# A decoder block on one core: at most six gathers in flight in the routed stage, no dots in its first groups, two activation tables asked for elsewhere, and small moves between engines

## The chip, the cores and the metric

The kernel runs on one core of a Trainium2 chip. The metric is the device time of one execution in microseconds (us). A core has five engines with a queue of instructions each: PE (TensorE, matrix products), DVE (VectorE), ACT (ScalarE), POOL (GpSimd) and SP, which here only issues transfers. Each engine runs its own row of instructions in order and waits on semaphores for the others. Sixteen DMA engines move data between HBM and the core's memory; transfers whose rows are picked by an index list (gathers) are issued by POOL.

## The reference, cut to what matters

One block on x of 256 tokens with 2048 columns: a projection, sparse attention beside a convolution, an output projection, a layer norm that gives y, and a channel mixer that picks 16 experts for each of 8 heads (128 choices per token) out of 128 x 128, and a second layer norm. The change touches the mixer and the two norms:

```python
def peer_ffn(y, wq, sub_keys, u_tab, v_tab):
...
        q = (yb @ wq).reshape(bsz, PEER_BLOCK, PEER_HEADS, 2, PK_HALF)
        s1 = jnp.einsum('bthd,hkd->bthk', q[..., 0, :], sub_keys[:, 0])
        s2 = jnp.einsum('bthd,hkd->bthk', q[..., 1, :], sub_keys[:, 1])
        v1, i1 = lax.top_k(s1, PK_TOPK)
        v2, i2 = lax.top_k(s2, PK_TOPK)
...
        top, pos = lax.top_k(cand, PK_TOPK)
        eidx = jnp.take_along_axis(cidx, pos, axis=-1)
        g = jax.nn.softmax(top.astype(jnp.float32), axis=-1)
        u = u_tab[eidx]
        v = v_tab[eidx]
        h = jax.nn.gelu(jnp.einsum('btd,bthkd->bthk', yb, u))
        return jnp.einsum('bthk,bthkd->btd', g * h, v).astype(y.dtype)
...
        ffn = peer_ffn(x, peer_wq[l], peer_keys[l], peer_u[l], peer_v[l])
        x = layer_norm(DN_ALPHA * x + ffn, ln2_g[l], ln2_b[l])
```

## The kernel before, in words

The work runs in stages, each with its own loop; times are those of the profiled execution.

1. *Front*, to 365 us: projection, attention, convolution. The change leaves it alone.
2. *y stage*, 365 to 390: the first layer norm by blocks of columns (the helpers called from L1320 to L1385), its transposes `yh` and `yl` for PE, made on ACT and DVE from PE's bank `yt`, the transposed keys `keyT`, and the first matmuls with wq (bank `pwq`). `prime` is a tile of one element per partition, written by small activations only.
3. *wq stage*, 390 to 480 (loop over h from L1395): queries and scores per head, the short lists, and from head 3 on the first gathers, as many as there are free buffers (L1431).
4. *Dense u stage*, 480 to 900 (loop over j = 0 to 127, L1567): `u_mult(j)` makes with 27 matmuls (L1473, L1474, L1477) the product of a dense part of all rows u (1152 columns) with y for one key; `u_keep` (L1480) copies it from PE's bank to W on ACT. The other 896 columns are gathered: `gather(i)` (L1125, POOL) fetches for each of 128 tokens the row of its i-th choice (i = 0 to 255: 128 choices by two token blocks), and `dot(i)` (L1135, DVE) multiplies it with y and sums it into one column of `hv`. `dots_until` (L1168) sets both into the rows of POOL and DVE. When the first 128 are done, `swap` (L1453) copies the y row of the second token block to `yp`. The softmax of the gates (`gate_softmax`, L1087) is a generator, of which the loop takes a step per j; behind it two transposes (L1518) turn the gates into columns.
5. *Routed stage*, 900 to 1081. What belongs to a token's choices is picked out of W and put back by products with hot matrices. A group q (0 to 63) is four tokens: `ext_hot` (L1621, PE) and `ext_relu` (L1626, ACT) make the hot matrix in a `slot`, `ext_mask` (L1630, PE) and `ext` (L1635, PE) fill a `bank`, `ext_max` (L1639, DVE) reduces it to `top`. The groups run in pairs to QP = 36, then singly and together with the second half of the work (`sc_hot` L1665, `sc_relu` L1671, `sc_val` L1677, `sc` L1683, `sc_keep` L1689 and L1691), which runs 37 groups behind. The last 56 gathers and 59 dots lie beside this. `x_dots(q, n)` (L1816) is called once per group: it places dots until `done` reaches n, with every third as a multiplication on POOL (L1805) and, four groups on, a sum on ACT (L1815), and then issues gathers into all free buffers (L1829). The buffers are the remaining `gu`, and `moreh`, `morel`, `gx` and `spare`. `due(q)` (L1841) is n: it spreads the dots that are left over the groups, with twice the pace behind group 37. All this is written out in program order (a manual schedule): the order of the Python code is the order on each engine.
6. *Dense v stage*, 1081 to 1553 (loop over j, L1995): `vr`, the dense rows of v, are split on ACT, DVE and POOL into `vh` and `vl` (L1748, L1753) for PE (L329 to L331); the other 768 columns are gathered (`gv`, L1708) and summed into `pg` on DVE (L1713). `pg` begins as a copy of `gacc` (L2002).
7. *Tail*, 1553 to 1578 (L2036 to L2110): the second layer norm for two token blocks tt, each of four column blocks: three from PE's banks, and `nb`, of 768 columns, from `pg`. `center` and `shift` do one on DVE, `aside` one on ACT and POOL (L2066 to L2068), `stats` and `moments` the mean and variance, `send` the output (L2084, SP's queue).

## Time and profile before

| | us |
|---|---|
| median of 3 runs | 1575.16 (1574.26 to 1581.13) |
| profiled execution | 1579.51 |
| its span in the trace | 1577.7 |
| PE busy | 1518.9 (96%) |
| DVE busy | 1350.9 (86%) |
| POOL busy | 1058.8 (67%) |
| ACT busy | 888.4 (56%) |

A row of the timeline has the start in us from the span's start, the duration, the engine, the line, the operation, what it writes and reads, how many instructions were merged, and in brackets the idle time of the engine ahead of it with what ended that. PEld is PE's weight load, beside PE. "issue" means that the profile shows nothing that was waited for. The granted clock is the share of full speed that PE was allowed.

### The profile page before, as it was taken

What the parts mean: (1) busy time and instruction counts of PE and PEld (TensorE: products, weight loads), DVE (VectorE), ACT (ScalarE), POOL (GpSimd) and SP (SyncE); (2) the same over time, 40 slices, a digit from 0 to 9 for tenths busy, and PEclk for the clock granted to TensorE, in tenths of its full rate; (3) what the DMA queues carried; (4) which work ended last, traced back from release to release, by engine and by line L of the source; (5) the groups of instructions that cost most, each with busy time, mean ns of one, the idle gap of its engine ahead of it and who ended that gap; (6) DMA issues with size and microseconds to landing.
All of it is one profiled execution on the core that took longest, in us unless ns stands there. A gap on an engine that the chain in (4) does not pass through costs nothing. (4 is left out here: it accounts for less than half of the span.)

```text
span 1577.7 us, 29654 instructions
## 1 busy us (share of the span) xinstructions
PE 1518.9 (96%) x10932; PEld 1387.6 (88%) x10932; DVE 1350.9 (86%) x2438; ACT 888.4 (56%) x1270; POOL 1058.8 (67%) x908
## 2 busy tenths in 40 slices
PE   9999999999999999999999979999999999999996
PEld 9998999988999999999999967777888888788885
DVE  5999687756778999999997778878989899999997
ACT  5445766545336777777777636776344443434443
POOL 1886000064887777777776678747888888888884
PEclk9999999999999999999999989999999999999998
DMA  9663535364758999999999987647999999999996
GB/s 346 226 247 134 179 111 189 106 233 158 282 172 306 393 386 387 384 392 381 397 383 375 321 269 233 208 159 220 389 382 386 386 391 382 376 380 386 393 389 246
DMA packets 101349, 475.78 MB, mean 302 GB/s; under 512 B 17712, under 2 KB 20372, under 8 KB 92628
## 3 DMA queue, kind: packets, MB, share of 16 engines
q1 hardware_dynamic: 59444, 253.21, 43.7%
q0 software_dynamic: 41040, 218.60, 37.1%
q8 instruction: 85, 1.39, 0.4%
q10 hardware_dynamic: 720, 2.10, 0.3%
q14 instruction: 60, 0.49, 0.1%
HBM read 468.99 MB, written 4.85 MB: 300 GB/s over the span
## 5 line engine op out<-in xcount | busy, mean ns | idle before, releaser
L1708 POOL DMA_INDIRECT gv<-in_v_rows_dram,e x256 | 298.7, 1167 | 66.5 <-issue 41.1
L1748 ACT ACTIVATE vh<-vr 128x1280 fp32r<-128x1280 f32 (+1 forms) x129 | 162.1, 1258 | 275.0 <-DMA vr<-in_v_dense_dram 199.7
L290 POOL TENSOR_TENSOR lo<-raw,hi 128x1024 fp32r<-128x1024 f32 (+1 forms) x84 | 189.1, 2271 | 158.4 <-ACT hi L272 157.8
L1473 PE MATMUL hp<-yh,uh 128*128 128x256 f32 x1152 | 282.5, 283 | 2.8 <-ACT W L1480 2.5
L1474 PE MATMUL hp<-yl,uh 128*128 128x256 f32 x1152 | 281.9, 283 | 0.0
L1125 POOL DMA_INDIRECT gu<-in_u_rows_dram,e x200 | 193.9, 970 | 115.9 <-DVE gu L1135 73.0
L1713 DVE SCALAR_TENSOR_TENSOR pg<-gv,hv,pg 128x768 f32<-128x768 f32 x247 | 251.8, 1019 | 4.3
L1473 PEld LDWEIGHTS hp<-yh,uh 128*128 128x128 f32 x1152 | 221.1, 192 | 3.5 <-ACT W L1480 2.9
L1135 DVE SCALAR_TENSOR_TENSOR gu<-gu,yp 128x896 f32<-128x896 f32 x200 | 211.2, 1079 | 14.1 <-DMA gu<-in_u_rows_dram,e 14.0
L330 PE MATMUL f<-vl,wh 128*128 128x512 f32 x512 | 209.2, 409 | 13.1 <-DVE vl L1753 9.3
L1474 PEld LDWEIGHTS hp<-yl,uh 128*128 128x128 f32 x1152 | 221.1, 192 | 0.0
L272 ACT ACTIVATE hi<-raw 128x1024 fp32r<-128x1024 f32 (+1 forms) x134 | 138.2, 1036 | 136.8 <-issue 25.4
L1190 ACT ACTIVATE uh<-ur 128x1152 fp32r<-128x1152 f32 x128 | 149.5, 1168 | 103.2 <-issue 61.1
L329 PE MATMUL f<-vh,wh 128*128 128x512 f32 x512 | 203.9, 398 | 2.0 <-ACT vh L1748 1.8
L331 PE MATMUL f<-vh,wl 128*128 128x512 f32 x512 | 202.4, 395 | 0.0
L1753 DVE TENSOR_TENSOR vl<-vr,vh 128x1024 fp32r<-128x1024 f32 (+1 forms) x129 | 159.5, 1237 | 35.3 <-ACT vh L1748 25.6
L1477 PE MATMUL hp<-yh,ul 128*128 128x256 f32 x1152 | 159.2, 283 | 0.0
L1477 PEld LDWEIGHTS hp<-yh,ul 128*128 128x128 f32 x1152 | 147.5, 192 | 0.1
L1195 DVE TENSOR_TENSOR ul<-ut,uh 128x768 fp32r<-128x768 f32 x126 | 119.9, 952 | 23.9 <-issue 10.4
L330 PEld LDWEIGHTS f<-vl,wh 128*128 128x128 f32 x512 | 99.5, 194 | 46.1 <-DVE vl L1753 22.0
L1196 POOL TENSOR_TENSOR ul<-ur,uh 128x384 fp32r<-128x384 f32 x128 | 132.7, 1037 | 6.8 <-ACT uh L1190 4.3
L1753 POOL TENSOR_TENSOR vl<-vr,vh 128x256 fp32r<-128x256 f32 (+1 forms) x129 | 118.6, 920 | 13.8 <-ACT vh L1748 11.3
(374 smaller groups left out, 3904.3 us busy)
## 6 DMA issues: line engine op xcount, KB each, us to landing
vr<-in_v_dense_dram SPq DMA_DIRECT2D x128, 640.0 KB
ur<-in_u_dense_dram SPq DMA_DIRECT2D x128, 576.0 KB
raw<-in_w_pieces_dram SPq DMA_DIRECT2D x62, 1024.0 KB
gv<-in_v_rows_dram,e POOLq DMA_INDIRECT x256
gu<-in_u_rows_dram,e POOLq DMA_INDIRECT x200
raw<-in_w_pieces_dram SPq DMA_DIRECT2D x5, 512.0 KB
raw<-in_w_pieces_dram SPq DMA_DIRECT2D x4, 608.0 KB
w1k<-in_cmp_w_dram SPq DMA_DIRECT2D x1, 2048.0 KB
```

The source lines that it names most:

```text
L290: e.tensor_tensor(lo[:, a:b], src[:, a:b], hi[:, a:b].bitcast(F32), op=OP.subtract)
L329: nc.tensor.matmul(acc, lhsT=ah, rhs=bh, start=start, stop=False)
L330: nc.tensor.matmul(acc, lhsT=ah, rhs=bl, start=False, stop=False)
L331: nc.tensor.matmul(acc, lhsT=al, rhs=bh, start=False, stop=stop)
L1125: nc.gpsimd.indirect_dma_start(out=gt, out_offset=None, in_=u_rows, in_offset=bass.IndirectOffsetOnAxis(ap=fl(e4, tt)[:, c:c + 1], axis=0))
L1135: nc.vector.scalar_tensor_tensor(gt, gt, 1.0, yr, op0=OP.mult, op1=OP.mult, accum_out=hv[:, tt, c:c + 1])
L1473: nc.tensor.matmul(hps[j], lhsT=uh[:, s], rhs=chunk(yh, k), start=k == 0, stop=False)
L1474: nc.tensor.matmul(hps[j], lhsT=uh[:, s], rhs=chunk(yl, k), start=False, stop=False)
L1477: nc.tensor.matmul(hps[j], lhsT=ul[:, s], rhs=chunk(yh, k), start=False, stop=k == UK - 1)
L1708: nc.gpsimd.indirect_dma_start(out=gvs[j, tt], out_offset=None, in_=v_rows_, in_offset=bass.IndirectOffsetOnAxis(ap=fl(e4, tt)[:, j:j + 1] ...
L1713: engine.scalar_tensor_tensor(pg[:, tt], gvs.pop((j, tt)), wv[:, tt, j:j + 1], pg[:, tt], op0=OP.mult, op1=OP.add)
L1753: e.tensor_tensor(vl, src[:, c], vh.bitcast(F32), op=OP.subtract)
```

## The change

- Routed stage: `x_dots` issues gathers only up to `done + 6` (before: into every free buffer), and `due` has no dots for the groups 0 to 3, and the same number over the rest. The u stage's last step (j = 127) places no dots and no gathers any more.
- Two one-element activations, Exp in the y stage and Gelu ahead of the last `u_keep`, are written into the code.
- wq stage: from head 3 on at most two gathers per half head.
- u stage: the copy in `swap` is DVE's; `gate_softmax` has one `yield` more, so that what follows it comes one j later.
- v stage: the split of row 1 stands ahead of the two `pg` copies in step 0.
- Tail: block 2 of the first token block goes from ACT and POOL to DVE, statistics of the second block come sooner, and the last addition is split, 512 columns on POOL and 256 on DVE, with two sends on ACT's queue.

```diff
+FLIGHT = 6
...
         yield
         yield
+        yield
...
         lows[2]()
+        nc.scalar.activation(prime, epst, AF.Exp)
...
                 if h >= 3:
-                    while room() and issued < min(EGS, len(indexed) * TOPK):
+                    for _ in range(min(2, room(), min(EGS, len(indexed) * TOPK) - issued)):
...
     def swap(tt):
-        nc.scalar.activation(yp, yrow.pop("held"), AF.Copy)
+        nc.vector.tensor_copy(yp, yrow.pop("held"))
...
-            dots_until(min(upto, routed, issued + CATCH), ending)
+            if j < P - 1:
+                dots_until(min(upto, routed, issued + CATCH), ending)
...
+        nc.scalar.activation(prime, epst, AF.Gelu_apprx_tanh)
         u_keep(P - 1)
...
-        while spare and issued < 2 * P:
+        while spare and issued < min(2 * P, done + FLIGHT):
...
         def due(q):
-            pace = q + 1 + PACE * max(0, q - LAG)
-            return min(2 * P, d0 + -(-u_left * pace // (NQ - 1 + PACE * (NQ - 2 - LAG))))
+            pace = max(0, q - 3) + PACE * max(0, q - LAG)
+            return min(2 * P, d0 + -(-u_left * pace // (NQ - 5 + PACE * (NQ - 2 - LAG))))
...
             if j == 0:
+                v_split(1)
                 for tt in range(2):
...
-            elif j + 1 < P and j != 1:
+            elif 1 < j < P - 1:
                 v_split(j + 1)
...
+        nc.gpsimd.tensor_tensor(zs[1][nb], zs[1][nb], gcol[nb], op=OP.mult)
+        nc.gpsimd.tensor_tensor(zs[1][nb][:, :512], zs[1][nb][:, :512], bcol[nb][:, :512], op=OP.add)
...
+        nc.vector.tensor_tensor(zs[1][nb][:, 512:], zs[1][nb][:, 512:], bcol[nb][:, 512:], op=OP.add)
+        for tt, b in ((0, 0), (0, nb), (0, 1), (0, 2), (1, 0), (1, 1), (1, 2)):
             send(tt, b)
+        for a, e in ((0, 512), (512, GC)):
+            nc.scalar.dma_start(out[P:, a:e], zs[1][nb][:, a:e])
```

The order on ACT in the y stage, before (`keyT`: transposed keys; `zn` and `mixb`: scaled columns of y; `yh`: transposed y; `hi`: the upper part of a piece of wq):

```order
L1233 ACTIVATE keyT<-kt_4471 128x512
L1233 ACTIVATE keyT<-kt_4477 128x512
L1273 ACTIVATE zn_4490<-yg,nmu,rs 128x512
L1273 ACTIVATE zn_4491<-yg,nmu,rs 128x512
L1294 ACTIVATE yh_4365<-yt_4509 128x4x128
L272 ACTIVATE hi_0_4516<-raw_4301 128x1024
L1273 ACTIVATE mixb_4372<-yg,nmu,rs 128x512
L1273 ACTIVATE mixb_4373<-yg,nmu,rs 128x512
L1294 ACTIVATE yh_4365<-yt_4551 128x128
```

and after, where lines are numbered 1 to 12 higher:

```order
L1235 ACTIVATE keyT<-kt_4477 128x512
L1349 ACT_TABLE_LOAD
L1349 ACTIVATE prime<-epst 128x1
L1275 ACTIVATE zn_4491<-yg,nmu,rs 128x512
L1275 ACTIVATE zn_4492<-yg,nmu,rs 128x512
L1296 ACTIVATE yh_4365<-yt_4510 128x4x128
L273 ACTIVATE hi_0_4517<-raw_4301 128x1024
L1275 ACTIVATE mixb_4372<-yg,nmu,rs 128x512
L1275 ACTIVATE mixb_4373<-yg,nmu,rs 128x512
L1793 ACT_TABLE_LOAD
L1793 ACTIVATE prime<-epst 128x1
L1296 ACTIVATE yh_4365<-yt_4552 128x128
```

Both small activations stand here, though the second is written 440 lines further down, and each has a table load; the loads further on, at the softmax and at the gelu, are in both orders.

The order on DVE at the start of the routed stage, before (`gu`, `moreh`: gathered rows; `top`: maxima of a group, two rows for a pair):

```order
L1135 SCALAR_TENSOR_TENSOR gu_68_11588,hv<-gu_68_11588,yp 128x896
L1135 SCALAR_TENSOR_TENSOR gu_69_11626,hv<-gu_69_11626,yp 128x896
L1135 SCALAR_TENSOR_TENSOR gu_70_11658,hv<-gu_70_11658,yp 128x896
L1639 TENSOR_REDUCE top<-bank_11688 128x4
L1639 TENSOR_REDUCE top<-bank_11689 128x4
L1135 SCALAR_TENSOR_TENSOR gu_71_11661,hv<-gu_71_11661,yp 128x896
L1639 TENSOR_REDUCE top<-bank_11690 128x4
L1639 TENSOR_REDUCE top<-bank_11691 128x4
L1135 SCALAR_TENSOR_TENSOR moreh,hv<-moreh,yp 128x896 x2
```

and after:

```order
L1137 SCALAR_TENSOR_TENSOR gu_66_11547,hv<-gu_66_11547,yp 128x896
L1643 TENSOR_REDUCE top<-bank_11684 128x4
L1643 TENSOR_REDUCE top<-bank_11685 128x4
L1643 TENSOR_REDUCE top<-bank_11686 128x4
L1643 TENSOR_REDUCE top<-bank_11687 128x4
L1137 SCALAR_TENSOR_TENSOR gu_67_11586,hv<-gu_67_11586,yp 128x896
L1137 SCALAR_TENSOR_TENSOR gu_68_11589,hv<-gu_68_11589,yp 128x896
L1643 TENSOR_REDUCE top<-bank_11684 128x4
L1643 TENSOR_REDUCE top<-bank_11685 128x4
L1137 SCALAR_TENSOR_TENSOR gu_69_11627,hv<-gu_69_11627,yp 128x896
```

The maxima of the first two pairs now stand ahead of the dots of gu 67 to 69 (gathers 195 to 197).

The order on POOL at the same place, before (L1125 gathers, L1805 multiplications):

```order
L1125 DMA gx_11677<-in_u_rows_dram,e_4150 128x896
L1125 DMA spare_11723<-in_u_rows_dram,e_4150 128x896
L1125 DMA spare_11737<-in_u_rows_dram,e_4150 128x896
L1125 DMA spare_11755<-in_u_rows_dram,e_4150 128x896
L1125 DMA moreh<-in_u_rows_dram,e_4150 128x896 x2
L1805 TENSOR_TENSOR morel<-morel 128x896
L1125 DMA gx_11674<-in_u_rows_dram,e_4150 128x896
L1125 DMA gx_11675<-in_u_rows_dram,e_4150 128x896
L1805 TENSOR_TENSOR gx_11676<-gx_11676,morel 128x896
```

and after:

```order
L1127 DMA gu_69_11627<-in_u_rows_dram,e_4150 128x896
L1127 DMA moreh<-in_u_rows_dram,e_4150 128x896 x2
L1127 DMA morel<-in_u_rows_dram,e_4150 128x896
L1127 DMA gx_11669<-in_u_rows_dram,e_4150 128x896
L1127 DMA gx_11670<-in_u_rows_dram,e_4150 128x896
L1127 DMA gx_11671<-in_u_rows_dram,e_4150 128x896
L1127 DMA gx_11672<-in_u_rows_dram,e_4150 128x896
L1810 TENSOR_TENSOR moreh<-moreh,morel 128x896
L1127 DMA spare_11760<-in_u_rows_dram,e_4150 128x896
L1127 DMA spare_11767<-in_u_rows_dram,e_4150 128x896
L1127 DMA spare_11785<-in_u_rows_dram,e_4150 128x896
L1810 TENSOR_TENSOR gx_11670<-gx_11670,morel 128x896
```

Before, thirteen gathers from gu 71 on stand ahead of the first multiplication and then two or so between two; after, seven behind gu 69, and then three.

More of the change, by code (lines that the diff above doesn't have):

```diff
@@ L2091, in tile_hybrid_block @@
         moments(0, 0)
-        for b in (nb, 2):
-            aside(0, b)
+        aside(0, nb)
         center(0, 1)
+        center(0, 2)
+        stats(1, 2)
+        stats(1, 0)
         shift(0, 0)
-        stats(1, 0)
-        shift(0, 1)
-        stats(1, 1)
-        stats(1, 2)
-        moments(1, 0)
-        aside(1, nb)
-        center(1, 1)
+        stats(1, 1)
+        moments(1, 0)
+        nc.scalar.activation(zs[1][nb], zb[1][nb], AF.Identity, bias=nm[:, 1:2], scale=rs[:, 1:2])
+        nc.gpsimd.tensor_tensor(zs[1][nb], zs[1][nb], gcol[nb], op=OP.mult)
+        nc.gpsimd.tensor_tensor(zs[1][nb][:, :512], zs[1][nb][:, :512], bcol[nb][:, :512], op=OP.add)
+        center(1, 1)
+        shift(0, 1)
+        shift(0, 2)
         shift(1, 0)
@@ L2106, in tile_hybrid_block @@
         shift(1, 2)
-        for tt, b in ((0, 0), (0, 1), (0, nb), (1, 0), (0, 2), (1, 1), (1, 2), (1, nb)):
+        nc.vector.tensor_tensor(zs[1][nb][:, 512:], zs[1][nb][:, 512:], bcol[nb][:, 512:], op=OP.add)
+        for tt, b in ((0, 0), (0, nb), (0, 1), (0, 2), (1, 0), (1, 1), (1, 2)):
             send(tt, b)
+        for a, e in ((0, 512), (512, GC)):
+            nc.scalar.dma_start(out[P:, a:e], zs[1][nb][:, a:e])
     manual.close()
```

## The prediction

> **What bounds the kernel now.** I read the page's head first, then a table of busy time by stage, then the timeline of each engine where PE, the TensorE, loses time.
>
> ```profile
> span 1577.7 us, 29654 instructions
> PE 1518.9 (96%) x10932; PEld 1387.6 (88%) x10932; DVE 1350.9 (86%) x2438; ACT 888.4 (56%) x1270; POOL 1058.8 (67%) x908
> ```
>
> PE is busy 96% of the span, so at most 59 us of waits can be won without taking matmuls away, and no edit here takes any. The table says where those waits lie. Its columns are the stretch, its length, the busy time of PE, PEld, DVE, ACT and POOL, then granted clock, DMA share and GB/s.
>
> ```profile
> 480.00:900.00 420.00, 416.29 (x3461) 415.33 (x3461) 391.03 (x828) 310.66 (x390) 310.07 (x312) 1.00 0.99 378
> 905.00:930.00 25.00, 15.51 (x92) 12.25 (x93) 15.11 (x27) 6.30 (x12) 16.97 (x17) 0.73 0.86 296
> 930.00:985.00 55.00, 53.83 (x451) 44.42 (x450) 47.35 (x85) 36.48 (x70) 44.61 (x37) 1.00 0.74 230
> 985.00:1040.00 55.00, 47.15 (x375) 39.65 (x375) 42.44 (x75) 37.81 (x76) 34.98 (x29) 0.94 0.69 224
> 1100.00:1550.00 450.00, 437.47 (x2161) 367.12 (x2161) 412.95 (x418) 186.34 (x180) 386.25 (x355) 1.00 1.00 384
> ```
>
> The dense u stage (480 to 900) loses 3.7 us in 420, with the DMA engines full at 0.99 beside PE. The dense v stage (1100 to 1550) has DMA at 1.00 and PE short of full: the transfers bound it, so time gained before it is carried to the end one to one, and nothing is gained inside it. The routed stage follows at once and loses 9.5 us within 905 to 930 and 7.9 within 985 to 1040, and in both the granted clock is below 1. So there are waits to win at the start and towards the end of the routed stage, little in the two dense stages, and what the last operations behind the v stage take.
>
> **The change part by part.**
>
> *Six in flight, no early dots.* The start of the routed stage, first PE, then POOL, then DVE:
>
> ```profile
> 911.49 1.18 PE L1630 MATMUL bank<-lines,fext 20*128 20x512 bf16 x2 [4.27 <-DVE top L1639]
> 926.34 1.07 PE L1621 MATMUL bank<-bt,lines 5*128 5x512 bf16 x2 [5.20 <-ACT slot L1626]
> ```
> ```profile
> 899.26 0.95 POOL L1125 DMA_INDIRECT gu<-in_u_rows_dram,e  x1 [0.30 <-DVE gu L1135]
> 900.79 0.94 POOL L1125 DMA_INDIRECT gu<-in_u_rows_dram,e  x1 [0.59 <-DVE gu L1135]
> 904.80 0.96 POOL L1125 DMA_INDIRECT gu<-in_u_rows_dram,e  x1 [3.06 <-DVE gu L1135]
> 907.73 0.94 POOL L1125 DMA_INDIRECT gu<-in_u_rows_dram,e  x1 [1.97 <-DVE gu L1135]
> ...
> 922.75 0.95 POOL L1125 DMA_INDIRECT moreh<-in_u_rows_dram,e  x1 [0.30 <-issue]
> ...
> 932.38 0.98 POOL L1125 DMA_INDIRECT morel<-in_u_rows_dram,e  x1 [0.16 <-ACT slot L1626]
> ```
> ```profile
> 906.36 1.09 DVE L1135 SCALAR_TENSOR_TENSOR gu<-gu,yp 128x896 f32<-128x896 f32 x1 [1.83 <-DMA gu<-in_u_rows_dram,e]
> 909.74 1.09 DVE L1135 SCALAR_TENSOR_TENSOR gu<-gu,yp 128x896 f32<-128x896 f32 x1 [0.47 <-DMA gu<-in_u_rows_dram,e]
> ```
>
> PE's first wait of 4.27 us is for the maxima (L1639) of the first groups, which stand behind the dots of the last gathers in DVE's row; and the dots wait for data, 1.83 and 0.47 us here. The order of after puts four maxima ahead of those dots, so this wait goes, with the half clock behind it (the two matmuls of 911.49 took 1.18 us). The second wait, 5.20 us, falls while POOL issues 13 gathers with 1.25 us from one to the next (907.73 to 922.75) and no multiplication between. In after the longest such row is eight (one gu, three more, four gx), later three. I take the first wait as gone and leave half a chance to the second.
>
> But PE does not simply gain both, since POOL is the next bound. Its multiplications in this stage as one group (busy, mean ns), and the end of the stage on POOL and PE:
>
> ```profile
> L1805 POOL TENSOR_TENSOR gx<-gx,morel 128x896 f32<-128x896 f32 x7 | 14.6, 2092 | 0.1
> ```
> ```profile
> 1015.16 0.95 POOL L1125 DMA_INDIRECT gx<-in_u_rows_dram,e  x1 [0.31 <-issue]
> ...
> 1026.12 0.98 POOL L1708 DMA_INDIRECT gv<-in_v_rows_dram,e  x1 [5.85 <-ACT slot L1671]
> ...
> 1029.12 0.39 PE L1665 MATMUL bank<-lines,fsc 20*128 20x512 bf16 x2
> ...
> 1031.42 0.40 PE L1665 MATMUL bank<-lines,fsc 20*128 20x512 bf16 x4
> 1035.61 1.65 PE L1683 MATMUL bank<-slot,slot 128*128 128x128 f32 x8 [3.79 <-ACT W L1691]
> ```
>
> In after, gather 197 is the last that waits for a gu buffer, the one of 900.79 above; gather 198 goes into other memory and can follow at 900.79 + 1.25 = 902.0. From there stand 58 gathers (198 to 255) and 18 multiplications in POOL's row, with the last gather at the end of it. A gather costs 1.25 (0.95 and an issue gap of 0.30); a multiplication 2.09 with 0.16 behind it, of which 0.3 stands in place of a gap, so 1.95 net. 58 x 1.25 + 18 x 1.95 = 107.6: the last gather is out at 1010 if POOL never waits. In this trace gathers issued at 899.26 and 904.80 were used at 906.36 and 909.74, that is 7.1 and 4.9 us later; so its dot is at 1016, and after the group of that dot and one more (the last groups are 2.30 apart, 1029.12 to 1031.42) the stage's last four hot matmuls, now at 1031.42, can stand at 1019 to 1020. I add 2 us of waits of POOL on data or buffers (bounds 0 and 8) and take **1021.5, a gain of 10** (4 to 14). The low end is where the second stall stays whole and POOL loses 8; the high end is where neither is so. The stop at 1035.61, 3.79 us of PE beside six gathers of gv in a row, is not touched by the change: POOL still sends those six together, and I keep it.
>
> A stage bound by POOL gives PE many small waits, and the clock has to be watched. PE once more, and the table for the 4 us behind:
>
> ```profile
> 987.15 1.16 PE L1683 MATMUL bank<-slot,slot 128*128 128x128 f32 x8 [2.12 <-ACT W L1691]
> ```
> ```profile
> 988.00:992.00 4.00, 4.00 (x23) 3.47 (x22) 2.25 (x5) 2.46 (x6) 2.93 (x4) 0.57 0.79 215
> ```
>
> After a wait of 2.12 us the clock was 0.57 for 4 us, some 1.7 us of matmul time lost. The same after each small wait of the new stage would lengthen PE's work, but only into time in which it waits for POOL. Without any wait or half clock PE would end near 1010 (1031.42 less waits of 9.5 + 1.2 + 4.1 by the table, and some 6 for the clocks of 0.73 and 0.94), so 1021.5 leaves it 11 us, room for six such stretches. The Trainium skill, TensorE: Matmul & The Clock Gate, "What's actually happening", has the clock halve after an idle window of about 3.4 us. By that rule waits of 2 us would cost nothing; the row above speaks against it, and the sum is the same by both.
>
> *Gate tables asked for sooner.* Two one-element activations (Exp, Gelu) are added. The order of after shows both in the y stage, Exp ahead of the two zn and Gelu ahead of the four yh, each with a table load, and the loads at the softmax and the gelu still stand, since the second displaces the first. So nothing is saved, and ACT gets two loads and two small operations more:
>
> ```profile
> 375.68 1.50 ACT L1273 ACTIVATE zn<-yg,nmu,rs 128x512 f32<-128x512 f32 x2
> 377.82 0.60 ACT L1294 ACTIVATE yh<-yt 128x512 fp32r<-128x512 f32 x1 [0.65 <-PE yt L1288]
> 381.21 1.21 ACT L1294 ACTIVATE yh<-yt 128x128 fp32r<-128x128 f32 x4 [0.47 <-PE yt L1288]
> 861.26 1.28 ACT L1093 ACT_TABLE_LOAD   x1
> ```
>
> A load is 1.28, the activation on one element I take at 0.2 (below the shortest row here, 0.60 for 512): 1.5 each, 3.0 in all. ACT's waits here, 0.65 and 0.47, absorb 1.1; DVE and PE behind ACT have no other cover, because the transposed y comes from ACT's yh. **+1.9** (0.8 if PE's buffered matmuls cover one load, 3.0 with no cover).
>
> The Trainium skill, ScalarE: Activation LUTs, "What ACT_TABLE_LOAD costs", puts a drain of about 1.38 us beside each load of 1.283. No drain shows in these rows; by that page the two would cost 5.3 us and my sum would be 2.3 us longer.
>
> *The swap on DVE, the transposes one step later.*
>
> ```profile
> 749.69 0.92 ACT L1453 ACTIVATE yp<-yrow 128x896 f32<-128x896 f32 x1 [1.75 <-DVE gu L1135]
> 751.21 0.39 PE L1473 MATMUL hp<-yh,uh 128*128 128x256 f32 x1 [1.26 <-ACT W L1480]
> 871.21 0.44 PE L1518 MATMUL colsg<-signs,gs 128*128 128x128 f32 x2 [0.93 <-issue]
> ```
>
> ACT waits 1.75 for DVE's last dot and copies 0.92 before it can empty PE's bank, and PE waits 1.26. On DVE the copy stands behind that dot anyway: the 1.26 goes, DVE gets some 0.9 more and had 29 us free in 420. The 0.93 of the transposes goes when the softmax has one step more. That is 2.2, but the DMA engines are 0.99 busy in this stage and the bytes stay the same, so I count half: **-1.2** (0.3 to -2.2).
>
> *Two gathers per half in wq.* The same gathers at other places, while POOL's splits go between; POOL's total there is unchanged: **0** (one gather's 1.25 either way).
>
> *The split of v row 1 ahead of the pg copies.*
>
> ```profile
> 1082.39 1.64 ACT L2002 ACTIVATE pg<-gacc 128x768 f32<-128x768 f32 x2
> 1083.97 1.25 ACT L1748 ACTIVATE vh<-vr 128x1280 fp32r<-128x1280 f32 x1
> 1085.27 0.50 PE L329 MATMUL f<-vh,wh 128*128 128x512 f32 x1 [0.55 <-ACT vh L1748]
> 1086.53 0.50 PE L330 MATMUL f<-vl,wh 128*128 128x512 f32 x1 [0.76 <-DVE vl L1753]
> ```
>
> The split starts 1.6 sooner and PE's 0.55 and 0.76 go, 1.3; the buffer of row 1 is free for the next transfer as much sooner. Little is put in front: the first gv sum waits for pg, and POOL has it behind two gathers. **-1.2** (0 to -1.6).
>
> *The tail.*
>
> ```profile
> 1570.09 0.73 POOL L2068 TENSOR_TENSOR z<-z,ln2b 128x256 f32<-128x256 f32 x1
> 1570.77 1.81 POOL L2067 TENSOR_TENSOR gacc<-gacc,ln2b 128x768 f32<-128x768 f32 x1
> 1572.66 1.80 POOL L2068 TENSOR_TENSOR gacc<-gacc,ln2b 128x768 f32<-128x768 f32 x1
> 1574.49 0.33 SPq L2084 DMA_DIRECT2D out_dram<-gacc  x1
> ```
>
> The last send waits for POOL's 1.80; with 512 of 768 columns it is 1.20, so 0.6 goes, as DVE's part of 256 lies beside it. The block of 256 that POOL had until 1570.8 goes to DVE, 0.3 at most, and statistics taken sooner give some tenths, while the sending moves to ACT's queue. **-1.1** (-0.3 to -1.8).
>
> Sum: -10 + 1.9 - 1.2 - 1.2 - 1.1 = -11.6. The profiled execution took 1579.51 with its span of 1577.7; the median of the runs is 1575.16, 0.3% less, so I take the difference off the median: about **1564 us**.
>
> **The rivals.**
>
> Slower: six in flight are too few. Between the issue of a gather and its multiplication, three dots on, stand six gathers and one multiplication, 9.5 us. With latency L, POOL waits (L - 9.5)/2 at each of 18 multiplications. For it speaks that the deeper queue of before hid any latency; against it the 4.9 and 7.1 us above at a DMA share of 0.86 to 0.91, while later stretches have 0.74 and 0.69. At L = 12 that is 22 us: last gather 1032, its dot 1044, the last hot matmuls 1048, 17 us later than now, and with the rest (-1.6) 1590. It decides from about 10.5 us on, where the stage ends as late as now.
>
> No change that can be told: the burst of eight still stalls DVE, POOL loses 8, and routed dots, squeezed into fewer groups, give 4 us only. Then -5.6, some 1570. For it: POOL's row is nearly full in before too, 107.4 us from 907.73 to its last gather at 1015.16.
>
> Faster still: all gaps go, the stop at 1035.61 with them, since its gathers would find PE further on: another 3.8 and about 1.5 of half clock, -17, 1558.
>
> The change does what its words say: the tables stay loaded. Then 1.28 at the softmax and as much at the gelu go, and the sum is nearer -15, 1560. The order speaks against it.
>
> **How the numbers follow.** The forecast has 0.51, the slower rival 0.08, the small gain 0.24, the larger 0.13, the tables 0.04. Half a per cent, 7.9 us, is about what a measurement of this kernel can tell from no change: faster means below 1567.3. The forecast's own range, from the bounds of its terms, is 1557 to 1571; nine tenths of it are faster. Faster: 0.46 + 0.13 + 0.03; same: 0.05 + 0.24; slower 0.08 and a rest of 0.01 for the unknown. The range takes in the larger and the small gain with their spread: 1555 to 1574; out of it fall the slower rival and the ends.
>
> **What would show it.** Right: PE without the 4.27 before the second pair's mask; POOL's gathers starting at 902 in threes between multiplications; the last four hot matmuls near 1021 by the old clock; two more table loads in the y stage and PE 1 to 3 us late there; no 1.26 at the swap; the last POOL addition 1.2 long. Wrong: POOL idle ahead of each multiplication, waiting for DMA (the slower rival); a stall of over 4 us still at the first burst; the later stages giving back what the routed stage gains.

## The result, and the profile after

| | before | after |
|---|---|---|
| median of the runs, us | 1574.71 (4 runs, 1573.01 to 1581.13) | 1557.74 (4 runs, 1553.55 to 1564.01) |
| profiled execution, us | 1579.51 | 1559.41 |
| its span, us | 1577.7 | 1557.6 |

The ratio of the runs is 0.9874 with a 95% interval of 0.9846 to 0.9903: 19.8 us (15 to 24) off 1575, where the forecast was 11.2. The two medians alone differ by 17.0. The sign was right and the size was not.

The first and the last matmul of the dense u stage (tile hp) and of the dense v stage (tile fboth) cut the span into stages. Before, then after; the two times in a row are the start of the first and of the last instruction of the group:

```profile
L1473 PE MATMUL hp<-yh,uh x1152: 278/283/387, 480.7 to 899.3; 128*128 128x256 f32 x192
L1477 PE MATMUL hp<-yh,ul x1152: 279/283/385, 482.9 to 900.5; 128*128 128x256 f32 x192
...
L329 PE MATMUL fboth<-vh,wh x256: 277/282/467, 1082.5 to 1561.2; 128*128 128x256 f32 x128
...
L331 PE MATMUL fboth<-vh,wl x256: 278/282/283, 1082.7 to 1561.4; 128*128 128x256 f32 x128
```
```profile
L1476 PE MATMUL hp<-yh,uh x1152: 278/283/385, 480.8 to 896.3; 128*128 128x256 f32 x192
...
L1480 PE MATMUL hp<-yh,ul x1152: 279/283/385, 483.1 to 897.5; 128*128 128x256 f32 x192
...
L330 PE MATMUL fboth<-vh,wh x256: 278/282/467, 1071.5 to 1541.5; 128*128 128x256 f32 x128
...
L332 PE MATMUL fboth<-vh,wl x256: 278/282/285, 1071.8 to 1541.7; 128*128 128x256 f32 x128
```

| stage, us | before | after | difference | forecast |
|---|---|---|---|---|
| to the first u matmul | 480.7 | 480.8 | +0.1 | +1.9 |
| u stage (to the last u matmul) | 419.8 | 416.7 | -3.1 | -1.2 |
| routed stage (to the first v matmul) | 182.0 | 174.0 | -8.0 | -10 |
| v stage (to the last v matmul) | 478.9 | 470.2 | -8.7 | -1.2 |
| tail | 16.3 | 15.9 | -0.4 | -1.1 |

Outside the v stage the sum is -11.4, where -10.4 was forecast. The surplus in these two traces is the 7.5 us by which the v stage missed its term.

*Start of the routed stage, after.* PE, then DVE and ACT, then POOL:

```profile
904.19 2.34 PE L1639 MATMUL bank<-W,slot 128*128 128x128 f32 x16
910.56 1.07 PE L1625 MATMUL bank<-bt,lines 5*128 5x512 bf16 x2 [4.03 <-ACT slot L1630]
```
```profile
902.69 0.69 DVE L1643 TENSOR_REDUCE top<-bank 128x4 f32<-128x512 f32 x1 [1.96 <-PE bank L1639]
908.47 0.69 DVE L1643 TENSOR_REDUCE top<-bank 128x4 f32<-128x512 f32 x1 [5.08 <-remote]
```
```profile
909.91 1.09 ACT L1630 ACTIVATE slot<-bank 128x512 f32<-128x512 f32 x2 [6.10 <-remote]
```
```profile
899.45 0.95 POOL L1127 DMA_INDIRECT moreh<-in_u_rows_dram,e  x1 [0.30 <-issue]
...
906.95 0.95 POOL L1127 DMA_INDIRECT gx<-in_u_rows_dram,e  x1 [0.30 <-issue]
909.07 2.09 POOL L1810 TENSOR_TENSOR moreh<-moreh,morel 128x896 f32<-128x896 f32 x1 [1.18 <-issue]
```

PE's first wait of 4.27 us for the maxima is gone. One stop of the second kind is left, 4.03 us; a stall of over 4 us at the first burst was on record as a sign of being wrong. DVE and ACT both wait there for matmuls that by their records were long over, and the profile can't name who released them ("remote"). In the trace's semaphore events PE's count stands still from 902.7 to 908.4 and then takes six steps by 910.1; the matmuls behind those steps are recorded one after the other from 902.3 to 906.5. I call this *held signals*. The profile models the ends of matmuls, so it can't tell a late signal from matmuls that ended later than recorded. It falls in a row of gathers that POOL issues without a break (898.20 to 907.90), as the stop of 5.20 us did before.

*y stage, after,* ACT:

```profile
375.78 1.28 ACT L1349 ACT_TABLE_LOAD   x1
377.07 0.20 ACT L1349 ACTIVATE prime<-epst 128x1 f32<-128x1 f32 x1
...
381.51 1.28 ACT L1793 ACT_TABLE_LOAD   x1
382.80 0.20 ACT L1793 ACTIVATE prime<-epst 128x1 f32<-128x1 f32 x1
...
387.01 1.20 ACT L1296 ACTIVATE yh<-yt 128x512 fp32r<-128x512 f32 x2
```

Two loads more, 1.48 with their activations, and the last yh of the stage stands at 387.01 where it stood at 385.33: +1.68.

*Tail, after:*

```profile
1550.71 1.80 POOL L2107 TENSOR_TENSOR gacc<-gacc,ln2b 128x768 f32<-128x768 f32 x1 [1.10 <-ACT gacc L2106]
1552.60 1.26 POOL L2108 TENSOR_TENSOR gacc<-gacc,ln2b 128x512 f32<-128x512 f32 x1
1553.89 0.86 ACTq L2120 DMA_DIRECT2D out_dram<-gacc  x2
```

The last addition is 1.26 in place of 1.80, but from its end to the end of the span there are 3.7 us with two sends on ACT's queue (1553.86 to 1557.6), 3.2 before with one on SP's (1574.46 to 1577.7).

### The profile page after: what moved, and what is told of

Same layout as the page of the kernel before. It is cut to its first block, busy times and chain, and to the rows that moved or that the text cites. A ratio compares the mean times of both kernels' runs of the same rounds, so it can differ in the third digit from the quotient of the medians.

```text
span 1557.6 us, 29640 instructions
## 1 busy us (share of the span) xinstructions
PE 1514.4 (97%) x10932; PEld 1387.5 (89%) x10932; DVE 1349.9 (87%) x2440; ACT 890.4 (57%) x1274; POOL 1050.5 (67%) x907
## 5 line engine op out<-in xcount | busy, mean ns | idle before, releaser
L1712 POOL DMA_INDIRECT gv<-in_v_rows_dram,e x256 | 287.9, 1125 | 65.2 <-issue 33.8
L1757 POOL TENSOR_TENSOR vl<-vr,vh 128x256 fp32r<-128x256 f32 (+1 forms) x129 | 121.9, 945 | 11.5 <-ACT vh L1752 9.3
```

What stands on the lines that cost most here:

```text
L1712: nc.gpsimd.indirect_dma_start(out=gvs[j, tt], out_offset=None, in_=v_rows_, in_offset=bass.IndirectOffsetOnAxis(ap=fl(e4, tt)[:, j:j + 1] ...
L1757: e.tensor_tensor(vl, src[:, c], vh.bitcast(F32), op=OP.subtract)
```

## The experiments

Runs that were measured together ran on one chip, and the chips differ. The kernel before takes 1577 to 1579 us on one chip, much as in the first measurement (1575; which chip that was isn't on record), and 1558 to 1561 on three others. A ratio is to the kernel before measured beside the run. The last five columns are stages, cut as above, in one trace each. The recorded expectations cut differently: they begin the v stage at the first matmul of tile f, some 1.5 us ahead of fboth, so their routed stage is 1.7 to 1.8 us shorter than here, and their v stage is some 17.5 us longer where it runs to the end of the span and some 6 where it runs to the last matmul of f.

| run | before, us | this, us | ratio (95%) | to u | u | routed | v | tail |
|---|---|---|---|---|---|---|---|---|
| *where before takes 1575 and more* | | | | | | | | |
| before, after (first traces) | 1574.7 | 1557.7 | 0.9874 (0.9846 to 0.9903) | 480.8 | 416.7 | 174.0 | 470.2 | 15.9 |
| b_again | 1579.0 | 1578.6 | 0.9997 (0.9975 to 1.0018) | 480.6 | 420.9 | 186.8 | 473.1 | 16.2 |
| b_third | 1577.1 | 1574.1 | 0.9990 (0.9966 to 1.0013) | 480.9 | 420.2 | 182.7 | 472.6 | 16.3 |
| b_due | 1577.1 | 1571.3 | 0.9959 (0.9940 to 0.9978) | 480.8 | 420.3 | 175.4 | 477.2 | 16.3 |
| b_flight | 1577.1 | 1566.6 | 0.9928 (0.9908 to 0.9947) | 481.1 | 418.4 | 174.9 | 474.9 | 16.3 |
| a_nosplit | 1579.0 | 1563.8 | 0.9888 (0.9834 to 0.9943) | 480.8 | 419.4 | 173.2 | 473.6 | 15.9 |
| a_flight16 | 1579.0 | 1561.9 | 0.9897 (0.9848 to 0.9945) | 481.0 | 418.6 | 171.1 | 470.4 | 15.9 |
| a_noprime | 1579.0 | 1558.2 | 0.9878 (0.9829 to 0.9927) | 479.4 | 417.5 | 169.9 | 468.9 | 15.9 |
| a_best | 1577.1 | 1559.9 | 0.9896 (0.9879 to 0.9913) | 479.4 | 417.2 | 173.5 | 471.0 | 15.9 |
| *other chips* | | | | | | | | |
| b_split | 1558.4 | 1558.9 | 1.0007 (0.9991 to 1.0022) | 481.4 | 419.9 | 169.0 | 475.0 | 16.3 |
| b_split2 | 1558.4 | 1556.4 | 0.9990 (0.9972 to 1.0008) | 480.7 | 419.0 | 167.3 | 471.7 | 16.3 |
| b_split3 | 1560.0 | 1557.9 | 0.9989 (0.9974 to 1.0004) | 481.1 | 420.1 | 168.9 | 472.3 | 16.3 |
| b_routed | 1560.9 | 1555.9 | 0.9968 (0.9949 to 0.9987) | 480.7 | 418.9 | 163.7 | 473.5 | 16.3 |
| b_routed2 | 1558.4 | 1553.8 | 0.9964 (0.9947 to 0.9981) | 480.8 | 418.2 | 162.9 | 470.3 | 16.3 |
| a_again | 1560.9 | 1552.4 | 0.9951 (0.9930 to 0.9971) | 481.3 | 417.1 | 162.8 | 474.5 | 15.9 |
| a_nosplit2 | 1558.4 | 1553.4 | 0.9969 (0.9948 to 0.9990) | 480.8 | 416.7 | 163.4 | 475.0 | 15.9 |
| a_noprime2 | 1560.0 | 1548.1 | 0.9916 (0.9896 to 0.9937) | 479.4 | 417.5 | 163.1 | 473.3 | 15.9 |
| a_pace1 | 1560.9 | 1556.0 | 0.9959 (0.9944 to 0.9974) | 480.7 | 417.3 | 167.9 | 472.4 | 15.9 |
| a_pace2 | 1560.9 | 1559.0 | 0.9984 (0.9968 to 0.9999) | 480.8 | 417.1 | 168.6 | 475.1 | 15.9 |

The theories at the start: the routed stage's gain is the removal of stops behind long rows of gathers (theory 1 of most runs), and the v stage's is the new place of the split, or chance.

**a_again: the changed kernel, no edit.**

> The changed kernel, unchanged. In the two traces so far the v stage (first matmul of row 0 to the end of the span) took 496.7 us before and 487.5 after, and nothing that I had forecast explains more than 2 of the 9. Theory 1: the rate of the transfers in the v stage differs from execution to execution; then the v stage of this run lies anywhere between 486 and 498, not at 487.5. Theory 2: the split of row 1 put ahead sets the stage's rhythm; then it is 487 to 488.5 again, and the time is 0.987 of before.

The v stage was 474.5, 4.3 longer than in the first trace, so its length is not fixed by the kernel. The routed stage was shorter instead. The same place as above, DVE, ACT and POOL:

```profile
903.34 0.69 DVE L1643 TENSOR_REDUCE top<-bank 128x4 f32<-128x512 f32 x1 [0.79 <-ACT slot L1630]
904.23 0.69 DVE L1643 TENSOR_REDUCE top<-bank 128x4 f32<-128x512 f32 x1 [0.20 <-PE bank L1639]
```
```profile
906.79 1.08 ACT L1630 ACTIVATE slot<-bank 128x512 f32<-128x512 f32 x2 [1.22 <-PE bank L1634]
```
```profile
899.94 0.96 POOL L1127 DMA_INDIRECT moreh<-in_u_rows_dram,e  x1 [0.30 <-PE bank L1625]
...
907.46 0.95 POOL L1127 DMA_INDIRECT gx<-in_u_rows_dram,e  x1 [0.30 <-issue]
908.75 2.08 POOL L1810 TENSOR_TENSOR moreh<-moreh,morel 128x896 f32<-128x896 f32 x1 [0.34 <-DMA moreh<-in_u_rows_dram,e]
914.48 2.10 POOL L1810 TENSOR_TENSOR gx<-gx,morel 128x896 f32<-128x896 f32 x1
...
1007.61 0.98 POOL L1127 DMA_INDIRECT spare<-in_u_rows_dram,e  x1 [0.16 <-issue]
```

The row of gathers is the same, and nothing is held: no wait is called remote. On this chip POOL's row sets the stage up to its last gather of u rows: from gather 198 (899.94) to the last (1007.61) it takes 107.7 us, where the prediction worked out 107.6 without waits. Multiplications are 5.73 apart here, three gathers and one multiplication. In the first trace of after the same stretch (899.45 to 1011.18) took 111.7.

**a_pace1, a_pace2: rows of gathers cut by waits.**

```diff
-        while spare and issued < min(2 * P, done + FLIGHT):
+        while spare and issued < min(2 * P, done + FLIGHT, i0 + q if q < 12 else 2 * P):
...
                 ext_max(q - 1)
+                if q < 12:
+                    nc.gpsimd.tensor_copy(prime, group(ha, q - 1)[:, :1])
...
+                if m < NQ - QP + 12:
+                    nc.gpsimd.tensor_copy(prime, group(W, m - 1)[:, 0, :1])
                 for job in jobs.pop(0):
```

The last of the three edits is in a_pace2 alone.

> POOL waits for the maxima of the pair before (a copy of one element) ahead of the gathers of the groups up to 10, and fewer gathers are allowed there, so that no more than three stand in a row. Theory 1: PE's signals are held back while POOL issues more than about four gathers one right behind the other; then PE's wait of 4.0 us at 910.6 and its half clock behind it go and group 12 starts 4 to 7 us sooner, of which the end of the stage keeps 0 to 3, since POOL's row is full behind it. Theory 2: the stop has another cause (data of the first gathers, or loads of the hot matrices that are late behind them); then a wait of some 4 us stays within the first ten groups, and the rest is as in the changed kernel or up to 2 us later for the gathers put off.

> As the run before, and the first six gathers of v rows are cut in the same way, by a wait for the groups put back before them. Theory 1: PE's wait of 2.1 us at 1025.7 and the half clock behind it (3.8 us for 16 matmuls in place of 2.1) go, 4 us at the start of the v stage. Theory 2: they stay, or move to the next place; the v stage starts where it does in the run before, or later by up to 2 us since the v rows come later.

The chip held no signals, so the stops that they were made against weren't there, and theory 1 was not tested. What they show is the price: POOL is the bound, its waits count, and the routed stage was 5.1 and 5.8 us longer than a_again's 162.8. A cure for held signals must not make POOL wait.

**b_routed, b_routed2: the three edits of the routed stage alone.** The kernel before with `FLIGHT`, the new `due` and no dots at j = 127, as in the diff above.

> The kernel before with only the limit of six, the four groups without dots and the last u step without dots. If the routed stage is a term of its own, it is 8 us shorter from the last u matmul to the first v matmul (180.2 before, 172.3 after, so 171 to 174 here), and front, wq and u stage are as before to 0.3 us. If the gain in the v stage hangs on the state in which the routed stage leaves the transfers, this run has it too (v stage about 487); by the split of row 1 it does not (about 496).

> The three edits of the routed stage together on the kernel before, a second time. On the chip where signals are held back the routed stage is 168 to 173 (limit alone 173.1, new dots alone 173.6, before 180 to 185), so the two parts do not add up; on the other chip 162 as before. Its v stage has the split where before has it: 479 to 485 by theory 1.

Routed 163.7 and 162.9, as in the changed kernel on such chips (162.8, 163.4, 163.1): the stage's gain needs nothing else. Front and wq are unchanged (480.7, 480.8). The u stage was 418.9 and 418.2, against 419.0 to 420.1 in the three b_split. That isn't the work of the last step without dots and gathers: the last five steps take 16.2 us in all twenty traces, and the difference arises before them. The three edits together without the rest weren't measured where signals are held.

The rows also say where the 5.3 us come from. Gathers 198 to 255 took 106.1 to 107.1 us in the three b_split as well, so POOL's row was full on these chips before the change. With the three edits it starts 1.9 us sooner behind the last u matmul, and the last group follows the last gather by 5.2 to 5.5 us in place of 9.7.

**b_again: the kernel before, no edit.**

> The kernel before, unchanged. On the chip of the last runs its time was 1560.9, 14 us less than where it was first measured, and the changed kernel showed no signals held back there. Theory 1: on such a chip the kernel before has no 4 to 5 us stops behind the rows of gathers either; its routed stage (last u matmul to first v matmul, 180.2 in the first trace) is then 163 to 168 us, against 161.1 of the changed kernel, and the change's gain in the routed stage is 2 to 6 us, not 8. Theory 2: the stops belong to the kernel before on every chip; then the routed stage is 178 to 181 again, and the v stage must be the shorter one. The v stage (496.7 in the first trace, 487.5 to 492.5 in the five others) tells whether its length hangs on the change: under chance 488 to 493 here, else 495 to 498.

It ran on the chip with held signals and can't show what the kernel before does without them; b_split does, below, whose routed stage has the same code. Its v stage was 473.1, 5.8 shorter than in the first trace of the same code: the first trace of before was a long one.

**a_nosplit, a_nosplit2, b_split, b_split2, b_split3: the split of v row 1.**

```diff
             if j == 0:
-                v_split(1)
                 for tt in range(2):
...
-            elif 1 < j < P - 1:
+            elif j + 1 < P and j != 1:
```

The diff is that of a_nosplit against the changed kernel; b_split is its opposite on the kernel before.

> The changed kernel with the split of v row 1 back behind the two pg copies. If the split is worth what I forecast, the second row's matmuls (the 64th matmul of its kind, 31.2 us behind the first in the changed kernel) come 1.2 later, 32.4, as in the kernel before (31.8). Where only the rate of the transfers counts, the v stage is 488 to 493 as in the other runs.

> The kernel before with only the split of v row 1 put ahead of the two pg copies. v stage from the first to the last v matmul: 476.4, 475.2, 476.7 and 477.2 in four kernels with the split ahead on the chip where before takes 1575, against 479.8 in the changed kernel without it and 478.8 to 485.2 in three runs of before; 478.6 to 481.3 with it on the other chip. Theory 1: the place of the split sets the rhythm of the whole stage; then 475 to 477.5 here, and the time is 3 to 6 us below before. Theory 2: the length is that of the transfers, by chance; then anywhere from 476 to 485, and the time within 2 us of before.

> The same kernel a second time, since one execution can't tell the two theories apart: under theory 1 both have a v stage of 475 to 477.5, under theory 2 the two differ by several us or lie where before lies.

> The changed kernel without that edit, a second time. Theory 1: its v stage is 479 or more again (479.8), and its time 3 us above the changed kernel. Theory 2: as likely below 478 as above.

> The kernel before with the split of v row 1 ahead, a third time. On the chips where before takes 1558 to 1561 the edit was worth nothing (v stage 481.3 and 478.0, ratios 1.0007 and 0.9990). If it counts on the chip where before takes 1575, the v stage is 475 to 477.5 there and the ratio 0.997 or less; if the length is chance, the ratio is 0.999 to 1.001 there too.

The matmul that these expectations count is the first of the ninth row, not of the second. In a_nosplit it came 31.4 us behind the first, against 30.9 in the first trace of after: 0.5 where I forecast 1.2. The edit alone is worth nothing that can be measured in the time: 1.0007, 0.9990, 0.9989, all on chips without held signals. PE's two waits at the start of the stage do go with it: the first rows of the changed kernel show none, in a_nosplit2 they are back. But most of that is given back two rows on, as in after (last line):

```profile
1063.71 0.50 PE L330 MATMUL f<-vh,wh 128*128 128x512 f32 x1 [0.51 <-ACT vh L1752]
...
1064.97 0.51 PE L331 MATMUL f<-vl,wh 128*128 128x512 f32 x1 [0.76 <-DVE vl L1757]
```
```profile
1083.20 0.51 PE L331 MATMUL f<-vl,wh 128*128 128x512 f32 x1 [1.46 <-DVE vl L1757]
```

It is the same in all twenty traces, to 0.1 us: counted from the first matmul of tile f, the third row starts at 7.4 with the split ahead and at 8.9 without it, the fifth at 16.5 and 17.0. From there on the traces scatter by more than the 0.5 that is left.

The stage waits for transfers: ACT's splits wait as long for the rows of v before (from 1100 to 1550) as after (from 1090 to 1530; total, times, longest), and PE is busy 463.9 us in the stage in both. Between the first and the last v matmul the amount is the same too, so the mean rate is the length said in another way:

```profile
ACT vh L1748 <- DMA vr<-in_v_dense_dram: 199.7, 90, 4.7
```
```profile
ACT vh L1752 <- DMA vr<-in_v_dense_dram: 199.1, 94, 4.6
```
```profile
DMA packets 38407, 180.59 MB, mean 378 GB/s; under 512 B 5985, under 2 KB 6061, under 8 KB 38370
```
```profile
DMA packets 38464, 180.64 MB, mean 385 GB/s; under 512 B 5998, under 2 KB 6118, under 8 KB 38428
```

Over all traces the stage is 468.9 to 478.9 us. On the other chips the kernels with the changed front half have 472.4 to 475.1, those on the basis of before 470.3 to 475.0: no difference. On the chip with held signals the five on the basis of before have 472.6 to 478.9 (mean 475.3) and the five changed ones 468.9 to 473.6 (mean 470.8). Parted by the split, the four with it ahead have 468.9 to 471.0 there and the six without it 472.6 to 478.9, with no overlap, which speaks for theory 1 on that chip. The times don't bear it out: a_nosplit's ratio (0.9888) lies between those of a_noprime and a_flight16 measured beside it (0.9878, 0.9897). The edit alone wasn't measured there. So what makes the 4.5 us, chance or the edit on that chip, stays open.

**a_noprime, a_noprime2: the two activations taken out.**

```diff
-        nc.scalar.activation(prime, epst, AF.Exp)
         y_bias(1)
...
-        nc.scalar.activation(prime, epst, AF.Gelu_apprx_tanh)
         u_keep(P - 1)
```

> The changed kernel without the two activations that ask for tables. The y stage ends 1.6 us sooner (as in the kernel before, 385.9). Theory 1: the 1.5 us that the changed kernel makes good in the wq stage come from the gathers at most two at a time; then the u stage begins 1.6 us sooner than in the changed kernel, at 479.2. Theory 2: the wq stage is bound by POOL, not by PE, and only swallows the delay; then the u stage begins at 480.7 as in both, and the time is the same to 0.3 us but for chance in the v stage. At the softmax ACT loads its table in both (no difference there).

> The changed kernel without the two activations that ask for tables, a second time, as the version that may beat both. The u stage begins 1.3 to 1.5 us sooner than in the changed kernel (479.4) and nothing else changes; ratio to before 0.994 on a chip where before takes 1560 (the changed kernel 0.9951), 0.987 where it takes 1575 (0.9874). By the rival, that the changed kernel's slower start is given back further on, the ratio is that of the changed kernel or above.

The u stage begins at 479.4 in both, 1.4 sooner than in the changed kernel and 1.3 sooner than before. So theory 1 of a_noprime holds: the gathers at most two at a time win 1.3 us in the wq stage, and the two activations take it back. Nothing further on is lost by leaving them out. The 1.4 us at the u stage are shown; that the time is better isn't. The ratio is 0.9916 (0.9896 to 0.9937) where the changed kernel had 0.9951 (0.9930 to 0.9971) on another chip, and 0.9878 where it had 0.9874.

**a_flight16: the limit lifted again.** `FLIGHT = 16` in place of 6.

> The changed kernel with up to 16 gathers in flight, so that the buffers are the only limit again, as before. If the limit of six is the part that counts, the row of gathers at the start of the routed stage grows from 8 to 11 or more and the first multiplication comes 3 to 4 us later; on a chip that holds signals back PE stops for 4 to 6 us or twice, the routed stage is 4 to 8 us longer. If only the place of the first dots counts, the routed stage is as in the changed kernel to 1 us (POOL has the same work), or 1 to 2 us shorter since data are never late.

Routed 171.1, not longer than 174.0 and 173.2 with the limit, so in this trace the limit isn't needed beside the new place of the dots. It did not make the long row that was expected: the row stayed at eight, since the next gather waited 4.52 us for a dot, and the first multiplication came at 920.48, in after at 909.07. So it doesn't test whether long rows hold signals.

**b_third, b_due, b_flight: one number of the routed stage each.** b_third is the kernel before; b_due has only the new `due`, b_flight only the limit.

> The kernel before, unchanged, as the measure for the two runs of this call that change one number of it each. Routed stage 180 to 185 us where signals are held back (first matmul of PE's second pair 4 to 6 us late), 163 to 168 where they are not; v stage 488 to 497.

> The kernel before with the new rule for the dots alone: none in the groups 0 to 3, as many gathers in flight as buffers allow, the last u step as before. Theory 1, the place of the first dots counts: PE's first wait for the maxima of the first pair goes, the routed stage is 6 to 10 us shorter than the kernel before on the same chip. Theory 2, the limit of six counts: under 3 us.

> The kernel before with the limit of six gathers alone. Theory 1, the place of the first dots counts: PE still waits some 4 us for the first maxima, the routed stage is within 3 us of the kernel before. Theory 2, the limit counts: 6 to 10 us shorter, and the longest row of gathers is 8.

Routed 175.4 and 174.9 against 182.7: with either part alone the stage is 7 to 8 us shorter on the chip with held signals, where I had one of them down for under 3. PE's waits in the first 30 us, b_third, b_due and b_flight:

```profile
912.59 1.18 PE L1630 MATMUL bank<-lines,fext 20*128 20x512 bf16 x2 [5.36 <-DVE top L1639]
927.07 1.07 PE L1621 MATMUL bank<-bt,lines 5*128 5x512 bf16 x2 [4.38 <-ACT slot L1626]
```
```profile
908.67 0.37 PE L1630 MATMUL bank<-lines,fext 20*128 20x512 bf16 x1 [1.46 <-DVE top L1639]
...
924.76 1.07 PE L1621 MATMUL bank<-bt,lines 5*128 5x512 bf16 x2 [6.83 <-ACT slot L1626]
```
```profile
910.40 1.17 PE L1631 MATMUL bank<-lines,fext 20*128 20x512 bf16 x2 [4.65 <-DVE top L1640]
918.91 0.37 PE L1622 MATMUL bank<-bt,lines 5*128 5x512 bf16 x1 [0.78 <-issue]
```

In these traces the two parts work on different stops. The place of the dots takes the first (5.36 to 1.46) and leaves the second (6.83); the limit takes the second (4.38 to 0.78) and leaves the first (4.65). The second half of that rests on one trace: the five changed kernels, four of them with the limit, have stops of 1.05 to 4.03 at that place. b_due had won only 2.3 us by group 12 and 2.6 by the last group; the other 4.7 came behind it, where its stop at the gv gathers was 1.50 and b_third's 3.71, and where its edit places no dots. So 2.6 is what the new place of the dots is shown to be worth alone. On the other chips the first stop is there in the kernel before, and the second is shorter (2.12 in b_split, 0.52 in b_split3, 1.10 in b_split2), b_split2:

```profile
910.55 1.17 PE L1630 MATMUL bank<-lines,fext 20*128 20x512 bf16 x2 [4.81 <-DVE top L1639]
926.73 0.86 PE L1621 MATMUL bank<-bt,lines 5*128 5x512 bf16 x2 [1.10 <-ACT slot L1626]
```

So the first stop is the kernel's, by its order of dots and maxima. The length of the second goes with the chip: "remote" waits of DVE or ACT stand in the routed stage of all ten traces where before takes 1575 and more, and in none of the ten others.

**a_best: each table asked for where ACT is free.**

```diff
+                if (h, half) == (2, 1):
+                    nc.scalar.activation(prime, epst, AF.Exp)
                 if half == 0:
                     wq_keys(h - 1, q0)
...
+            if q == 0:
+                nc.scalar.activation(prime, W[:, 0, P - 1:P], AF.Gelu_apprx_tanh)
             for p in (q, q + 1):
                 ext(p)
```

The basis is a_noprime.

> The changed kernel with each table asked for where nothing waits for ACT: Exp in the wq stage, where ACT is busy 33 of 90 us, and Gelu behind the hot matrices of the first groups, with an input that is not there sooner; in the y stage none. Each table is then loaded once, as in the kernel before. Against the changed kernel: -1.4 in front of the u stage (as measured without the two activations), -0.8 to -1.5 at the softmax, where no load stands any more, and at group 32, where PE waited 2.6 behind the gelu's load, up to -2.6, less what POOL's row gives back. Sum -2 to -5, ratio to before 0.985 or less on a chip where before takes 1575 or more, 0.992 where it takes 1561. Rival: ACT's first slots of the routed stage wait for the load, 1.3 us there, and the sum is -1 to -3.

The load in the wq stage costs nothing (u begins at 479.4), and no load stands at the softmax any more, but the u stage is 417.2 against a_noprime's 417.5, a difference within the scatter, so nothing can be seen of a load there. Of the wait that I had put down to the gelu's load 2.40 us are still there without it. The expectation of 0.985 or less was missed: the ratio is 0.9896 (0.9879 to 0.9913), not told from the 0.9878 (0.9829 to 0.9927) of a_noprime.

## Why the prediction was wrong, point by point

**The v stage (-1.2, measured -8.7 in the two traces).** This is the step that failed. "The transfers bound it, so time gained before it is carried to the end one to one, and nothing is gained inside it" took the stage's own length as fixed, and then gave 1.2 to the split against its own rule. The runs show both wrong. The split wins 1.5 us by the third row, has 0.5 left by the fifth, and alone left no mark in the time on the two chips where it was measured. And the length isn't fixed: without an edit the kernel before had 478.9, 473.1 and 472.6, the changed one 470.2 and 474.5. One profiled execution of a transfer-bound stage is a sample, and the first trace of before, at 478.9, was the longest of twenty. Of the 8.7 us, 4.5 remain in the means of five and five traces where before takes 1575 and more, and none on the other chips; their cause is open.

**The sum by the means.** Those ten traces give 0 to the start of the u stage (without a_noprime and a_best, which lack the two activations of the change), -2.0 in it, -11.5 in the routed stage (there against the three without an edit), -4.5 and -0.4: -18.4, where -11.6 was forecast. Half of the missing 6.8 is the v stage's, the rest the start of the u stage (1.9), the routed stage (1.5) and the u stage (0.8), less 0.7 in the tail. That the first two traces put the whole surplus into one stage was chance in part. The bounds of the terms, added straight, reach from 0.4 to 20 us off; "1557 to 1571" is narrower, and the prediction gives no reason for that.

**The routed stage (-10, measured -8.0, and -11.5 in the means where signals are held).** Before has 182.0, 186.8 and 182.7 there, the five changed kernels 169.9 to 174.0, so 183.8 to 172.3 in the mean. The mechanism held in the main: the first wait went, POOL's row bounds the stage and took 107.7 us where it was not held up, and six in flight were never too few. The hot matmuls forecast for 1021.5 came at 1019.4; by the old clock, with the u stage's 3.0 us, that is 1022.4. They are not the stage's last, as the prediction has it (the second half of the work goes on to 1077.07 before), but what stands behind them was only 1.1 us longer after. What I had not seen is that the "remote" waits go with the chip, and that POOL's row was full before the change where they are missing. There the same edits win 5.3 us (168.4 to 163.1 in the means), not 10. The stop at the gv gathers, which I kept at 3.79, was 2.14 after.

**The u stage (-1.2, measured -3.1).** "I count half", because the DMA engines are 0.99 busy, was wrong. In spite of that share PE sets this stage: of 417 us it is busy 415.9, and forty steps (22 to 61) take 129.6 us in all twenty traces.

```profile
480.00:897.00 417.00, 415.92 (x3462) 415.44 (x3463) 394.65 (x860) 309.98 (x389) 309.40 (x313) 1.00 0.99 382
```

So the gain at the swap came whole: the two steps there take 8.0 us in each of the ten traces with ACT's copy and 6.5 in each of the ten with DVE's. The transposes' 0.93 went too: nine of the ten without that edit have a wait there, up to 0.97, and none of the ten with it. But nine of the ten changed traces lose 0.5 us in the first ten steps, for a reason that stays open, and PE's wait at the softmax is anything from nothing to 2.2 us. Over all traces the stage is 419.6 and 417.5 in the mean, -2.1; the other 1.0 of the -3.1 is the pair's.

**The tables (+1.9, measured +1.7 in the y stage, 1.4 at the u stage).** Right, by the rows of the loads: 1.28 + 0.20 each, less the waits that they filled. The Trainium skill, ScalarE: Activation LUTs, "What ACT_TABLE_LOAD costs", has a drain of 1.38 us beside each load; none shows here, and the 1.68 measured for two loads leaves no room for it.

**Two gathers per half (0, measured -1.3).** Outside the bound of 1.25 by little, and of the wrong kind: the total on POOL is the same, but PE waits for the splits (lo) that stand behind the third gather in POOL's row, and with two they come sooner. Of PE's three waits for them before (0.79, 0.54, 0.52) a_noprime has only the first, 0.78.

**The tail (-1.1, measured -0.4).** The shorter addition came as forecast, 0.54, and what stands ahead of it was some 0.4 shorter; behind it 0.5 was lost with two sends on ACT's queue in place of one on SP's, which I had left out.

**The rivals.** Six in flight too few: in the two traces of the changed kernel shown here the first POOL multiplication waited 1.18 and 0.34 us, the other seventeen not at all. A burst of eight that still stalls: it did, for 4.03 us, but the stage did not lose 8. All gaps gone (-17): not the mechanism, though the time came near, which was luck. The tables stay loaded: no, as the order said (its sum is -14.2, not -15).

## What to carry to other kernels

A term read from one trace is only as firm as the stage is repeatable: take several executions, on several chips, of a stage bound by transfers, before its length enters a sum. Ask for each wait whether its releaser is named: what the kernel's order causes comes back on each chip, what is put down to "remote" may not. And where an engine is about to become the bound, work out its row alone; that number, 107.6 against 107.7, was the best of the prediction. And compare stages step by step: the 1.5 us of the swap and the 0.5 of the split stand in every trace, in stages whose lengths vary by several us.

## What the runs showed of the hardware

- One kernel, without an edit, takes 1558 to 1561 us on three chips and 1575 to 1579 on another and in the first measurement (1.2% more). Some 15 us of it lie in the routed stage (183.8 against 168.4 in the means; the latter from b_split, which has the same code there).
- Where it takes longer, DVE and ACT wait for PE's signals without a named releaser, and PE's count stood still for 5.7 us in after, in stretches in which POOL issues several gathers one right behind the other; on the three other chips the same rows of gathers hold nothing. That the gathers cause it was argued from the place and not shown.
- The granted clock was 0.50 behind PE waits of over 4 us (from 911.5 to 916.6 in before, from 910.6 to 916.1 in after), which by an estimate (half of such a stretch) costs 2.6 to 2.8 us more than the wait. The length of the wait alone doesn't decide: the clock was 0.57 for 4 us behind one of 2.12 us in before and 0.50 for 3.4 us behind one of 1.10 in b_split2, and stayed at 1.00 behind one of 2.31 at 1001 in a_nosplit2. The Trainium skill, TensorE: Matmul & The Clock Gate, "What's actually happening", has an idle window of 3.4 us for it; the waits of 1.10 and 2.12 us were shorter.
